# Moving the first key lists into the query projection and changing the pace of gathered rows in a PEER encoder layer

## The chip, the cores and the metric

The kernel runs on one core of a Trainium2 chip, as one launch. The metric is the time of one execution on the device in microseconds (us). A core has a matrix engine (TensorE, in the profile PE, its weight loads PEld), VectorE (DVE), ScalarE (ACT), GpSimd (POOL) and SyncE (SP, used here only to issue transfers), each with an instruction queue of its own that it works off in order, and 16 DMA engines that all transfer queues share.

## What is computed

One layer of an encoder on 512 tokens of width 1024, in float32. Cut to the part that matters here:

```python
h = h + W_out [ DiffAttn(xn) || BiRG-LRU(xn) ]
q = (xn @ wq).reshape(B, S, 8, 2, 64)             # 8 heads, two half keys
s1, s2 = q[..., 0, :] . keys1, q[..., 1, :] . keys2   # 128 scores each
v1, i1 = top_k(s1, 16);  v2, i2 = top_k(s2, 16)
cand = v1[..., :, None] + v2[..., None, :]        # 256 candidates a head
sc, pos = top_k(cand, 16);  g = softmax(sc)
logits = xn . exp_u[idx];  act = gelu(logits) * g # 8 x 16 rows of 16384 experts
h = h + act . exp_v[idx]
h = h + sigmoid(rms(h) W_g) * (p W_p);  out = rms(h)
```

## The kernel before

The 512 tokens are four tiles of 128. A float32 product is made from three matmuls on split operands: `split` (L90 and L92) writes the rounded high part on ACT and the rest on DVE, `mm3` (L97 to L99) issues high x high, high x low, low x high.

The experts are looked up in two ways. Tiles 0 to 2 are **dense**: all 16384 rows of u pass through TensorE in 128 blocks (the first sweep; `u_mm` writes a block's logits `lg`), and then all rows of v in 128 blocks (the second sweep; `v_mm` sums into six PSUM banks `acc`). What makes this right is a weight matrix that is zero but for the chosen experts; it is built from the key lists with one-hot products (`build`, PSUM tile `pg`), written to DRAM as `gd` and read back as `gc` in the second sweep (`weights`, L994: eight parts for a group of eight blocks, 192 KB each). Tile 3 is **gathered**: its 128 rows of u and 128 rows of v for each token are fetched by indirect DMA from POOL (`gather`, L888, 128 rows of 4 KB for one index column), and DVE takes one dot product (L920) or one weighted sum into h (L927) for each. 256 such gathers are spread over both sweeps and the end.

The order is written out by hand. The query projection runs head by head (loop at L864): 24 matmuls a head, the split of the result into `qh`, `ql`, the load and split of the weights two heads ahead. Beside it, two steps of the key lists (`topk`, L687) of tile 3 are issued a head. In `topk`, a head's scores are one PSUM tile `pk`, copied by ACT to `sc`; two steps of five DVE instructions each (L700 to L704) then find the 16 largest of both halves. After the eight heads follow the candidate lists, the softmax (an Exp on ACT, L738), and the arithmetic of the indices. The lists of tiles 0, 1 and 2 follow in the first sweep. There each block calls three generators with a budget in units (`Background.run`): `top` (the lists), `make` (the builds) and `side` (the gathered rows, 1.15 units each):

```python
    for j in range(P):
        advance()                       # row_load up to three blocks ahead
        ...
        u_mm(*ahead.pop(0), lg)
        first = not res[0]              # lists of tile 0 not done yet
        top.run(TOP_FIRST if first else TOP_THEN)
        make.run(MAKE_2 if top.done else MAKE)
        ...
        side.run(SIDE_1 if first else SIDE if not make.done or (vp is not None and parts) else SIDE_2)
```

At block 118 at the latest the build is finished by force, its room is handed on (`settle`), and the first group of `gc` is loaded in four blocks, two parts each. A scheduler then orders the instructions of each engine by their dependencies, so that a line may stand far from its place in the code. At the end `bg.run(1e9)` works off what is left of the gathered rows, before the last part of tile 3 (`finish`).

Of the kernel before, what the change touches and what calls it, by code (L numbers as in the profile page):

```python
# [11 lines left out]
F32 = mybir.dt.float32  # L12
# [4 lines left out]
U32 = mybir.dt.uint32  # L17
# [5 lines left out]
P = 128  # L23
# [3 lines left out]
NT = T // P  # L27
EPS = 1e-6
HEADS = 8
K = 16  # L30
# [9 lines left out]
KEEP = 30  # L40
G_SCALE = 2.0 ** 14
RO_AT = [2, 1, 1, 1, 1, 1, 1, 0, 0, 1, 0, 0, 1, 0, 0, 1, 0, 0, 1, 1, 9]
TOP_FIRST, TOP_THEN, MAKE, SIDE_1, SIDE, BG_V, PREP, SIDE_2 = 1.9, 1.0, 0.57, 0.85, 1.2, 1.2, 60, 2.1
MAKE_2, REST = 0.62, 3
LAST = 3
N_HOT = 13
# [14 lines left out]
def trunk(ctx, tc, x, xT, pT, pos, w_lru, w_qkv, w_out, w_q, keys, wab, w_gate, w_proj,  # L61
          vec, row, ut, u, v, out, dbg=None):
# [26 lines left out]
    def split(src, hi, lo, scale=None):  # L89
        nc.scalar.activation(hi, src, AF.Copy, scale=1.0 if scale is None else scale)  # L90
        if scale is None:
            return nc.vector.tensor_sub(lo, src, hi.bitcast(F32))  # L92
        else:
            return nc.vector.scalar_tensor_tensor(lo, src, scale, hi.bitcast(F32), op0=ALU.mult, op1=ALU.subtract)
# [27 lines left out]
    def wq_load(hd):  # L122
        w = nw.tile([P, DK, P], F32, tag="w", name="w")
        nc.sync.dma_start(w, w_q[hd])
        wh = nw.tile([P, DK, P], R, tag="wh", name="wh")
        wl = nw.tile([P, DK, P], R, tag="wl", name="wl")
        split(w, wh, wl)
        return wh, wl
# [13 lines left out]
    def q_mm(ps, wh, wl, half):  # L142
        ts = slice(0, T) if half is None else slice(half * T // 2, (half + 1) * T // 2)
        for k in range(DK):
            mm3(ps[:, ts], wh[:, k, :], wl[:, k, :], x2h[:, k, ts], x2l[:, k, ts], k == 0, k == DK - 1)

    with ExitStack() as st:
        res = st.enter_context(tc.tile_pool(name="res", bufs=1, reuse_waits="tile"))
# [128 lines left out]
        for ct in range(8):  # L277
# [12 lines left out]
            if ct < 4:  # L290
# [16 lines left out]
                for da in range(4):  # L307
                    i = da * 4 + ct
# [86 lines left out]
        for blk in range(3):  # L395
            accs = []

            for t in range(NT):
                tag = ((), ("ro", "po"), ("tr", None, None, "tr"))[blk][t:t + 1]
# [5 lines left out]
            for k2 in range(4):  # L405
# [5 lines left out]
                for kk in range(2):  # L411
                    k = 2 * k2 + kk
# [235 lines left out]
    def row_load(src):  # L648
        r = up.tile([P, D], F32, tag="r", name="r", bufs=3)
        nc.sync.dma_start(r, src)  # L650
        rh = up.tile([P, D], R, tag="rh", name="rh", bufs=3)
        rl = up.tile([P, D], R, tag="rl", name="rl", bufs=3)
        pace.append(split(r, rh, rl))
        return rh, rl
# [9 lines left out]
    bp = e0.enter_context(tc.tile_pool(name="bp", bufs=1, reuse_waits="tile"))  # L664
# [22 lines left out]
    def topk(t, res):  # L687

        tt = slice(t * P, (t + 1) * P)
        v12 = bp.tile([P, 2, HEADS, K], F32, tag="v12", name="v12", bufs=1)  # L690
        i12 = bp.tile([P, 2, HEADS, K], U32, tag="i12", name="i12", bufs=1)
        for hd in range(HEADS):
            pk = psb.tile([P, 2, P], F32, tag="tr", name="pk", bufs=2)
            mm3(pk, qh[:, hd, tt], ql[:, hd, tt], kh, kl, True, True)
# [161 lines left out]

    res = {t: [] for t in range(NT)}

    def tops():
        for t in list(range(NT - 1, ND_V - 1, -1)) + list(range(ND_V)):  # L860
            yield from topk(t, res[t])

    tg = tops()
    for hd in range(HEADS):  # L864
        if hd + 2 < HEADS:
            wq.append(wq_load(hd + 2))
        if hd < 2:
            ps = pq[hd]
            q_mm(ps, *wq[hd], 1)
        else:  # L870
            ps = psb.tile([P, T], F32, tag=("ro", "po")[hd % 2], name="ps")
            q_mm(ps, *wq[hd], None)
        split(ps, qh[:, hd, :], ql[:, hd, :])
        for _ in range(2 if hd else 0):
            next(tg)
    nx.close()
    bw = e0.enter_context(tc.tile_pool(name="bw", bufs=2, side="right", reuse_waits="tile"))

    pace, after = [], []

    def behind(ins):

# [65 lines left out]
    def builds():  # L948
        for t in range(ND_V):
            while not res[t]:  # L950
                yield None
            yield from build(t, *res[t][0])

    def rest():
        for t in range(ND_V, NT):
            while not res[t]:
                yield None
            yield from rows(uv_items(t))
# [14 lines left out]
                    self.debt -= c  # L973

    top, make, side = Background(tg), Background(builds()), Background(rest())

    JC = 8
    J0 = (P - KEEP) // JC * JC
    order = [(J0 + i) % P for i in range(P)]
    feed = [ut[j].rearrange("p k e -> p (k e)") for j in range(P)] + [v[j * P:(j + 1) * P, :] for j in order]  # L980
    ahead = []
    kept = {}

    def advance():
        while feed and len(ahead) < 3:
            ahead.append(row_load(feed.pop(0)))

    def weights(c, part, vp):

        if part == 0:  # L990
            gcs.append(vp.tile([P, NTB, JC, TB], F32, tag="gc", name="gc"))
        b0, b1 = part * NTB // JC, (part + 1) * NTB // JC
        j = order[c * JC]
        ld_ = nc.sync.dma_start(gcs[-1][:, b0:b1], gd[b0:b1, :, j * TB:(j + JC) * TB].rearrange("b p (j t) -> p b j t", t=TB))  # L994

# [14 lines left out]
    sv = ctx.enter_context(ExitStack())  # L1010
    vp, gcs, built, parts = None, [], None, list(range(JC))
    for j in range(P):
        advance()
        if vp is not None:

# [4 lines left out]
        else:  # L1020
            if j == P - KEEP:
                top.run(1e9)
            i = j - (P - KEEP)
# [154 lines left out]
    bg = Background(side.gen)  # L1178
    prep = Background(prepare())
    advance()  # L1180
    vn = [v_prep(0)]

    for i in range(P - LAST + 1):
        advance()
        if i + 1 < P:
            vn.append(v_prep(i + 1))
        if i == P - JC:
            load_gains()
        if i == P - LAST:
            break  # L1190
        rhl, ahl = ahead.pop(0), vn.pop(0)
        for t in range(ND_V):
            v_mm(i, t, *rhl, *ahl)
        if i >= PREP and not prep.done:
            prep.run(BG_V)
        else:
            bg.run(BG_V)
# [114 lines left out]
```

## Time and profile before

| | |
|---|---|
| median of 3 runs | 1486.02 us (1483.64 to 1488.97) |
| the profiled execution | 1491.43 us, of which the span from first to last instruction 1489.7 |
| PE busy | 1462.2 us, 98% of the span |
| DVE, ACT, POOL busy | 1246.7 us (84%), 737.3 (49%), 375.3 (25%) |
| moved by DMA | 392.64 MB, mean 264 GB/s |
| query projection, first sweep, second sweep | about 250 to 295, 295 to 890, 890 to 1430 us of the span |

Busy time of PE is the union of matmuls that overlap in the pipeline, so short pauses between them don't show in it; they show in the number of matmuls that fall into a stretch, and in what PE waited for. An engine's idle time matters only where PE waits for it.

### The profile page before, as it was taken

What the parts mean: (1) busy time and instruction counts of PE and PEld (TensorE: products, weight loads), DVE (VectorE), ACT (ScalarE), POOL (GpSimd) and SP (SyncE); (2) the same over time, 40 slices, a digit from 0 to 9 for tenths busy, and PEclk for the clock granted to TensorE, in tenths of its full rate; (3) what the DMA queues carried; (4) which work ended last, traced back from release to release, by engine and by line L of the source; (5) the groups of instructions that cost most, each with busy time, mean ns of one, the idle gap of its engine ahead of it and who ended that gap; (6) DMA issues with size and microseconds to landing.
All of it is one profiled execution on the core that took longest, in us unless ns stands there. A gap on an engine that the chain in (4) does not pass through costs nothing.

```text
span 1489.7 us, 22160 instructions
## 1 busy us (share of the span) xinstructions
PE 1462.2 (98%) x7907; PEld 1294.2 (87%) x7907; DVE 1246.7 (84%) x2382; ACT 737.3 (49%) x1059; POOL 375.3 (25%) x320
## 2 busy tenths in 40 slices
PE   9999999999999999999999999999999999999997
PEld 7888678899999999999999997888888888888876
DVE  7686986798999998999888777888887568988896
ACT  7974654253455665556455533333333553333346
POOL 0000000002222263333433352232222004344350
PEclk9999999999999999999999999999999999999999
DMA  7134012158788899888997899899999789999962
GB/s 259 59 97 128 14 62 97 46 166 290 247 289 314 306 338 326 305 320 306 345 360 274 286 364 330 294 332 320 360 359 347 253 267 335 370 375 379 345 205 78
DMA packets 168047, 392.64 MB, mean 264 GB/s; under 512 B 15232, under 2 KB 89728, under 8 KB 164864
## 3 DMA queue, kind: packets, MB, share of 16 engines
q1 hardware_dynamic: 111760, 206.74, 41.0%
q0 software_dynamic: 38464, 140.00, 26.5%
q10 hardware_dynamic: 17712, 44.48, 7.8%
q8 instruction: 62, 1.02, 0.3%
q14 instruction: 49, 0.40, 0.1%
HBM read 344.63 MB, written 46.53 MB: 263 GB/s over the span
## 4 chain that ended last, share of the span: by engine, by line
PE 71%; DVE 14%; issue 5%; DMA 5%; ACT 4%; POOL 1%; SPq 0%; DVEq 0%; POOLq 0%; ACTq 0%
PE acc L99 11%; PE acc L98 11%; PE acc L97 11%; PE psl L97 7%; PE psl L99 7%; PE psl L98 7%; DVE rl L92 3%; PE pg L849 2%; PE ps L97 2%; PE ps L99 2%; PE ps L98 2%; DVE h L927 1%; DMA rr<-in_u_dram,qidx 1%; DMA r<-in_v_dram 1%; DVE rr L920 1%
## 5 line engine op out<-in xcount | busy, mean ns | idle before, releaser
L90 ACT ACTIVATE rh<-r 128x1024 fp32r<-128x1024 f32 x256 | 271.2, 1060 | 460.2 <-PE psl L98 190.2
L92 DVE TENSOR_TENSOR rl<-r,rh 128x1024 fp32r<-128x1024 f32 x256 | 312.4, 1221 | 104.0 <-ACT rh L90 103.3
L97 PE MATMUL psl<-x2h,rh 128*128 128x384 f32 x1024 | 346.8, 339 | 1.1 <-ACT lg L661 0.8
L99 PE MATMUL psl<-x2h,rl 128*128 128x384 f32 x1024 | 343.3, 335 | 2.6 <-DVE rl L92 2.6
L98 PE MATMUL psl<-x2l,rh 128*128 128x384 f32 x1024 | 343.0, 335 | 0.0
L97 PE MATMUL acc<-rh,ah 128*128 128x512 f32 x768 | 299.9, 391 | 2.5 <-ACT ah L90 2.5
L99 PE MATMUL acc<-rh,al 128*128 128x512 f32 x768 | 300.1, 391 | 1.2 <-DVE al L92 1.2
L98 PE MATMUL acc<-rl,ah 128*128 128x512 f32 x768 | 299.6, 390 | 0.0
L888 POOL DMA_INDIRECT rr<-in_u_dram,qidx x84 | 109.0, 1298 | 356.6 <-DVE rl L92 284.9
L99 PEld LDWEIGHTS psl<-x2h,rl 128*128 128x128 f32 x1024 | 192.4, 188 | 3.3 <-DVE rl L92 3.3
L97 PEld LDWEIGHTS psl<-x2h,rh 128*128 128x128 f32 x1024 | 192.2, 188 | 1.6 <-ACT lg L661 1.1
L98 PEld LDWEIGHTS psl<-x2l,rh 128*128 128x128 f32 x1024 | 192.6, 188 | 0.0
L888 POOL DMA_INDIRECT rr<-in_v_dram,qidxv x82 | 123.5, 1507 | 222.6 <-DVE rl L92 185.8
L97 PEld LDWEIGHTS acc<-rh,ah 128*128 128x128 f32 x768 | 144.7, 188 | 33.6 <-ACT ah L90 3.8
L99 PEld LDWEIGHTS acc<-rh,al 128*128 128x128 f32 x768 | 144.5, 188 | 32.7 <-DVE al L92 3.1
L98 PEld LDWEIGHTS acc<-rl,ah 128*128 128x128 f32 x768 | 144.6, 188 | 30.1
L920 DVE CUSTOM_DVE_ANT_0 rr<-rr,xn 128x1024 f32<-128x1024 f32 x84 | 102.0, 1217 | 8.7 <-DMA rr<-in_u_dram,qidx 8.7
L927 DVE SCALAR_TENSOR_TENSOR h<-rr,qg,h 128x1024 f32<-128x1024 f32 x82 | 104.9, 1279 | 0.1
L852 ACT COPY sg<-pg 128x512 f32<-128x512 f32 x96 | 96.0, 1109 | 6.4 <-PE pg L849 5.5
L888 POOL DMA_INDIRECT xn<-in_v_dram,qidxv x46 | 68.6, 1492 | 118.5 <-DVE rl L92 107.9
L90 ACT ACTIVATE ah<-am 128x384 fp32r<-128x384 f32 x128 | 65.6, 513 | 53.9 <-DVE am L1061 27.8
L888 POOL DMA_INDIRECT xn<-in_u_dram,qidx x44 | 62.8, 1427 | 113.0 <-DVE rl L92 82.4
(338 smaller groups left out, 2215.5 us busy)
## 6 DMA issues: line engine op xcount, KB each, us to landing
r<-in_ut_dram SPq DMA_DIRECT2D x128, 512.0 KB, 4.7
r<-in_v_dram SPq DMA_DIRECT2D x128, 512.0 KB, 6.8
gd<-sg ACTq DMA_DIRECT2D x24, 1024.0 KB, 7.8
gc<-gd SPq DMA_DIRECT2D x128, 192.0 KB, 5.0
ld<-lg ACTq DMA_DIRECT2D x98, 192.0 KB, 5.4
lg<-ld SPq DMA_DIRECT2D x98, 192.0 KB, 6.5
w<-in_w_qkv_dram SPq DMA_DIRECT2D x12, 512.0 KB, 3.6
w<-in_w_out_dram SPq DMA_DIRECT2D x8, 512.0 KB, 3.7
```

The source lines that it names most:

```text
L90: nc.scalar.activation(hi, src, AF.Copy, scale=1.0 if scale is None else scale)
L92: return nc.vector.tensor_sub(lo, src, hi.bitcast(F32))
L97: nc.tensor.matmul(ps, lhsT=lh, rhs=rh, start=first, stop=False)
L98: nc.tensor.matmul(ps, lhsT=lh, rhs=rl, start=False, stop=False)
L99: nc.tensor.matmul(ps, lhsT=ll, rhs=rh, start=False, stop=last)
L849: nc.tensor.matmul(pg[:, i - q, :], lhsT=o1[:, i // 2, :, i % 2], rhs=o2[part][:, i // 2, :, i % 2], start=part == 0, stop=part == 1)
L852: nc.scalar.copy(sg[:, :, s0:s0 + 4].rearrange("p j t -> p t j"), pg)
L888: g = nc.gpsimd.indirect_dma_start(out=dst, out_offset=None, in_=table, in_offset=bass.IndirectOffsetOnAxis(ap=idx, axis=0))
L920: behind(nc.vector.tensor_tensor_reduce(rr, rr, xn[:, t, :], 1.0, 0.0, ALU.mult, ALU.add, act[:, k % 16:k % 16 + 1]))
L927: behind(nc.vector.scalar_tensor_tensor(h[:, t, :], rr, qg[:, t, k:k + 1], h[:, t, :], op0=ALU.mult, op1=ALU.add))
```

## The change

The lists of all four tiles get a generator of their own (`tks`). In each of the heads 1 to 7 of the query projection one step of tile 0 is issued behind the two of tile 3; `v12` and `i12` get two buffers so that two tiles can be under way. In the heads 5 to 7 one block of u each is loaded and split (`row_load`), which the first sweep did before. Two budgets change: while tile 0's lists are unfinished a block's share of gathered rows rises from 0.85 to 1.0, and after the builds it falls from 2.1 to 1.6. The work is the same in all.

```diff
-TOP_FIRST, TOP_THEN, MAKE, SIDE_1, SIDE, BG_V, PREP, SIDE_2 = 1.9, 1.0, 0.57, 0.85, 1.2, 1.2, 60, 2.1
+TOP_FIRST, TOP_THEN, MAKE, SIDE_1, SIDE, BG_V, PREP, SIDE_2 = 1.9, 1.0, 0.57, 1.0, 1.2, 1.2, 60, 1.6
@@ topk
-        v12 = bp.tile([P, 2, HEADS, K], F32, tag="v12", name="v12", bufs=1)
-        i12 = bp.tile([P, 2, HEADS, K], U32, tag="i12", name="i12", bufs=1)
+        v12 = bp.tile([P, 2, HEADS, K], F32, tag="v12", name="v12", bufs=2)
+        i12 = bp.tile([P, 2, HEADS, K], U32, tag="i12", name="i12", bufs=2)
@@ before the query projection
+    tks = {t: topk(t, res[t]) for t in range(NT)}
+
     def tops():
         for t in list(range(NT - 1, ND_V - 1, -1)) + list(range(ND_V)):
-            yield from topk(t, res[t])
+            yield from tks[t]
 
     tg = tops()
+    pace, after = [], []
+
+    JC = 8
+    J0 = (P - KEEP) // JC * JC
+    order = [(J0 + i) % P for i in range(P)]
+    feed = [ut[j].rearrange("p k e -> p (k e)") for j in range(P)] + [v[j * P:(j + 1) * P, :] for j in order]
+    ahead = []
+
+    def advance():
+        while feed and len(ahead) < 3:
+            ahead.append(row_load(feed.pop(0)))
+
     for hd in range(HEADS):
...
         for _ in range(2 if hd else 0):
             next(tg)
+        if hd:
+            next(tks[0])
+        if hd >= HEADS - 3:
+            ahead.append(row_load(feed.pop(0)))
```

The moved definitions (`pace`, `JC`, `order`, `feed`, `ahead`, `advance`) are taken out further down. Behind the change the lines of the gathered rows are L937 and L944 (before L920 and L927), that of the `gc` loads L1001 (before L994).

On DVE, in the query projection behind the split of head 1 (`v_2356` holds the lists of tile 3, `v_2374` those of tile 0), the instructions stand so:

```order
 L703 MAX v_2356<-sc 128x8 x2
 L704 MAX_INDEX i_2357<-v_2356,sc 128x8 x2
+L700 MAX v_2374<-sc 128x8 x2
+L701 MAX_INDEX i_2375<-v_2374,sc 128x8 x2
+L702 MATCH_REPLACE sc<-v_2374,sc 128x128 x2
+L703 MAX v_2374<-sc 128x8 x2
+L704 MAX_INDEX i_2375<-v_2374,sc 128x8 x2
 L92 TENSOR_TENSOR wl<-w,wh 128x1024
 L92 TENSOR_TENSOR ql<-ps,qh 128x512
```

A pair of tile 0's steps has come in ahead of the split of the next weights. It comes in at every second head, four times in all. The scheduler makes the seven steps into four full pairs, and they are gone from the first sweep. The three splits of u (`rl`) stand at the same place in both kernels, ahead of the query projection.

On SP's queue, at the end of the first sweep (`r` is a block of u or v, `gc` a part of the weights):

```order
-L650 DMA r<-in_ut_dram 128x1024 x20
-L994 DMA gc<-gd 128x3x128 x6
+L650 DMA r<-in_ut_dram 128x1024 x18
+L1001 DMA gc<-gd 128x3x128 x2
 L650 DMA r<-in_ut_dram 128x1024
-L994 DMA gc<-gd 128x3x128 x2
+L1001 DMA gc<-gd 128x3x128 x2
+L650 DMA r<-in_ut_dram 128x1024
+L1001 DMA gc<-gd 128x3x128 x2
+L650 DMA r<-in_ut_dram 128x1024
+L1001 DMA gc<-gd 128x3x128 x2
 L650 DMA r<-in_ut_dram 128x1024 x3
```

Six parts of `gc` that stood in one piece behind block 123 now stand in pairs, the first behind block 121.

On DVE, around the splits of the blocks 125 to 127 of u (`rl`), before:

```order
L92 TENSOR_TENSOR rl_9135<-r_9132,rh_9134 128x1024
L920 ISA xn_76,act0_69<-xn_76 128x1024
L920 ISA act0_69 128x1
L920 ISA rr_9051,act0_69<-rr_9051,xn_76 128x1024
L920 ISA act0_69 128x1
L92 TENSOR_TENSOR rl_9171<-r_9168,rh_9170 128x1024
L920 ISA rr_9088,act0_69<-rr_9088,xn_76 128x1024
L920 ISA act0_69 128x1
L920 ISA rr_9092,act0_69<-rr_9092,xn_76 128x1024
L920 ISA act0_69 128x1
L92 TENSOR_TENSOR rl_9208<-r_9205,rh_9207 128x1024
```

and behind the change, from the same block on:

```order
L92 TENSOR_TENSOR rl_9144<-r_9141,rh_9143 128x1024
L937 ISA rr_9027,act0_69<-rr_9027,xn_76 128x1024
L937 ISA act0_69 128x1
L92 TENSOR_TENSOR rl_9179<-r_9176,rh_9178 128x1024
L937 ISA xn_76,act0_69<-xn_76 128x1024
L937 ISA act0_69 128x1
L937 ISA xn_76,act0_69<-xn_76 128x1024
L937 ISA act0_69 128x1
L92 TENSOR_TENSOR rl_9217<-r_9214,rh_9216 128x1024
```

Between the splits stand fewer gathered rows. From the split of block 125 of u to that of the fourth block of v there are 12 before and 9 behind the change. In all, 18 rows instead of 19 are left behind the last split of v.

## Rows read from the trace of the kernel before

**Rows 1.** The page: busy time and share of the span.
```profile
PE 1462.2 (98%) x7907; PEld 1294.2 (87%) x7907; DVE 1246.7 (84%) x2382; ACT 737.3 (49%) x1059; POOL 375.3 (25%) x320
```

**Rows 2.** Busy time by stretch: us, PE, PEld, DVE, ACT, POOL (instructions), PEclk, DMA share, GB/s.
```profile
890.00:915.00 25.00, 21.71 (x85) 16.30 (x84) 16.95 (x27) 7.95 (x12) 7.73 (x7) 0.93 0.99 363
915.00:1430.00 515.00, 514.53 (x2272) 425.56 (x2271) 415.54 (x551) 200.01 (x274) 153.68 (x125) 1.00 0.94 328
```

**Rows 3.** What PE waited for, 340 to 860 us (total, times, longest).
```profile
PE psl L99 <- DVE rl L92: 2.6, 2, 1.4
PE pg L849 <- DVE o L834: 1.5, 2, 1.3
PE psl L97 <- ACT lg L661: 0.8, 1, 0.8
```

**Rows 4.** What was waited for around the change of sweeps, 895 to 912 us.
```profile
ACT rh L90 <- DMA r<-in_v_dram: 10.9, 2, 5.5
...
PE acc L97 <- ACT ah L90: 2.1, 2, 1.7
```

**Rows 5.** DVE in order of time, query projection: start, us, instruction [idle before].
```profile
245.99 3.49 DVE L92 TENSOR_TENSOR rl<-r,rh 128x1024 fp32r<-128x1024 f32 x3
...
271.54 1.23 DVE L92 TENSOR_TENSOR wl<-w,wh 128x1024 fp32r<-128x1024 f32 x1 [1.65 <-ACT wh L90]
...
277.36 1.23 DVE L92 TENSOR_TENSOR wl<-w,wh 128x1024 fp32r<-128x1024 f32 x1 [1.65 <-ACT wh L90]
```

**Rows 6.** DVE in order of time, lists of tile 0 in the first sweep.
```profile
344.33 0.48 DVE L700 MAX8 v<-sc 128x8 f32<-128x128 f32 x2
...
346.68 1.20 DVE L920 CUSTOM_DVE_ANT_0 rr<-rr,xn 128x1024 f32<-128x1024 f32 x1
...
347.81 1.22 DVE L92 TENSOR_TENSOR rl<-r,rh 128x1024 fp32r<-128x1024 f32 x1
348.94 0.48 DVE L700 MAX8 v<-sc 128x8 f32<-128x128 f32 x2
```

**Rows 7.** What DVE waited for, 342 to 530 us.
```profile
DVE rr L920 <- DMA rr<-in_u_dram,qidx: 0.8, 1, 0.8
```

**Rows 8.** ACT in order of time, lists of tile 0.
```profile
348.16 1.06 ACT L90 ACTIVATE rh<-r 128x1024 fp32r<-128x1024 f32 x1 [2.85 <-PE psl L98]
...
352.71 1.06 ACT L90 ACTIVATE rh<-r 128x1024 fp32r<-128x1024 f32 x1 [2.85 <-PE psl L98]
...
375.44 1.06 ACT L90 ACTIVATE rh<-r 128x1024 fp32r<-128x1024 f32 x1 [2.85 <-PE psl L98]
...
379.60 1.06 ACT L90 ACTIVATE rh<-r 128x1024 fp32r<-128x1024 f32 x1 [2.72 <-PE psl L98]
...
389.92 0.31 ACT L738 ACTIVATE qg<-qg 128x128 f32<-128x128 f32 x1 [3.05 <-DVE qg L737]
```

**Rows 9.** SP in order of time, end of the first sweep.
```profile
850.41 7.20 SPq L994 DMA_DIRECT2D gc<-gd  x6
857.71 1.94 SPq L650 DMA_DIRECT2D r<-in_ut_dram  x1
```

**Rows 10.** The chain that ended last: start, us, what.
```profile
888.94 15.64 DMA r<-in_v_dram
```

**Rows 11.** The page: DMA issues (KB each, median us to landing).
```profile
r<-in_v_dram SPq DMA_DIRECT2D x128, 512.0 KB, 6.8
```

**Rows 12.** DMA from 885 to 905 us: all, and the gathers' queue.
```profile
DMA packets 3763, 7.68 MB, mean 384 GB/s; under 512 B 296, under 2 KB 2191, under 8 KB 3762
...
q0 software_dynamic: 1306, 4.76, 61.3%
```

**Rows 13.** The end: DVE, ACT in order of time; PE's waits, 1455 to 1490 us.
```profile
1460.17 1.28 DVE L927 SCALAR_TENSOR_TENSOR h<-xn,qg,h 128x1024 f32<-128x1024 f32 x1
...
1461.49 1.06 ACT L1142 ACTIVATE x<-h 128x1024 f32<-128x1024 f32 x1 [0.26 <-DVE h L927]
...
PE gate L97 <- DVE hl L92: 1.4, 1, 1.4
```

More of the change, by code (lines that the diff above doesn't have):

```diff
@@ L875, in trunk @@
             next(tg)
+        if hd:
+            next(tks[0])
+        if hd >= HEADS - 3:
+            ahead.append(row_load(feed.pop(0)))
     nx.close()
     bw = e0.enter_context(tc.tile_pool(name="bw", bufs=2, side="right", reuse_waits="tile"))
-    pace, after = [], []
     def behind(ins):
@@ L975, in trunk @@
     top, make, side = Background(tg), Background(builds()), Background(rest())
[L977 to L981, printed above, removed]
     kept = {}
-    def advance():
-        while feed and len(ahead) < 3:
-            ahead.append(row_load(feed.pop(0)))
     def weights(c, part, vp):
```

## The prediction

> **What bounds the kernel now.** I read the busy times first. PE is busy 98% of the span [rows 1], and the change moves PE's work about without removing any, so it can win only time in which PE issues slower than it could. That is found by counting matmuls in stretches. In the quiet second sweep 2272 instructions fall into 515 us, one in 0.227 us; in the 25 us in which the sweeps change hands only 85, where 110 would fit [rows 2]. The 25 that are missing are worth 25 x 0.227 = 5.7 us, with the clock at 0.93 of full speed among the causes. Before that, from 340 to 860 us, PE waited 4.9 us in all: 2.6 for the low part of a block of u, 1.5 for a one-hot operand, 0.8 for a PSUM bank that ACT had not emptied [rows 3]. So the reader is to see a kernel whose front half is even and which has one hole, at the change of sweeps, plus the end.
>
> The hole is a transfer. PE waits for ACT's rounded weights, and ACT for blocks of v, twice, up to 5.5 us [rows 4]: ACT works in order, and the weights that PE needs stand behind the next block's split. The chain that ended last goes through one block of v that was issued at 888.94 and took 15.64 us to land [rows 10], where the median of such a block is 6.8 [rows 11]. From 885 to 905 us the engines move 384 GB/s, and 4.76 of 7.68 MB belong to the gathers [rows 12]. The blocks of v stand in line with the gathered rows of tile 3.
>
> **The change, part by part.**
>
> The splits of three blocks of u: nothing. They stand at the same place of DVE's order and of SP's before and after, and the trace has them in one piece at 246 us, ahead of the query projection [rows 5]. Their cover is the end of the attention stage, which is not touched.
>
> Four pairs of list steps beside the query projection: nothing there. One pair costs DVE 2.35 us, from 344.33 to 346.68 [rows 6]. A head lasts 5.82 us, of which DVE waits 1.65 for ACT [rows 5], so it works 4.2; with a pair at every second head it works 6.5 and 4.2 in turn, 5.3 on the mean. The split that is delayed by 0.7 us is that of weights for the head after the next, and PE reaches those a whole head later. Queued behind the added pair on DVE are that split and the split of the last head's result; on ACT one more copy a pair. If the cover failed, each pair would cost 0.7 us, 2.8 in all. PE's products for four more heads only move: a block with one lasts 4.55 us, without 4.16 [rows 8], so PE spends 1.6 us there and saves them later.
>
> The front of the first sweep: plus 2.0 us. Here DVE is full: from 342 to 530 us it waited once, 0.8 us [rows 7]. A split and a gathered row take it 1.13 us each [rows 6]. Up to the softmax of tile 0 it now has 4 pairs, 4 splits and 2 gathered rows less, 9.4 + 4.5 + 2.3 = 16.2 us; but PE gets there four blocks sooner, 18.2 us. So DVE comes 2.0 us later as seen from PE. PE's 1.6 us in the projection give about 1.0 of that back, the part that DVE doesn't need for the fourth pair. ACT waits 3.05 us for DVE at this Exp [rows 8], and PE's 0.8 us for the bank [rows 3] hang on it; it should wait about 1 us longer. Then one more gathered row than before falls in front of the first build, 1.1 us more, which is paid at the next tight place, the wait for u in the lists of tile 1. Ends: nothing, if the blocks that are split ahead absorb it, and 3.5, if all of 2.0 + 1.1 arrives and a bit of clock with it. I take 2.0, because DVE has no pause in which to catch up.
>
> The change of sweeps: minus 4.7 us. From the split of block 125 of u to the fourth of v, six blocks or 25 us, DVE consumes 9 gathered rows instead of 12, and a gather is issued when DVE frees its buffer. A gather moves as much as a block, 0.524 MB (the same 128 rows of 4 KB) [rows 11]. Wanted before: 6 blocks and 12 gathers, 9.4 MB in 25 us, 378 GB/s, and some 47 GB/s for a part of weights (192 KB) in each block: 425. Delivered: 384 [rows 12]. Wanted after: 315 + 47 = 362. Besides, the six parts of weights that kept SP busy for 7.2 us, with a block of u behind them for 1.94 more [rows 9], now go in pairs from two blocks earlier, so that the stage is entered without arrears. The block that is late need not be punctual: at 15.64 us it cost 4 us of waiting, so about 11 would do. Ends: 5.7 won, if the hole closes, and nothing. I leave 1.0 in it, because the blocks v1 and v2 keep two gathered rows each.
>
> *The page's limit.* The Trainium skill (DMA: Bandwidth & Descriptors, section Where 436 GB/s comes from) gives about 358 GB/s as what HBM grants one core. This trace does not agree, with 384 over 20 us in that stage [rows 12]. By 358 the 362 wanted would still be too many, the term would shrink to about nothing, and the sum would be plus 0.8.
>
> The end: minus 1.2 us. 18 gathered rows are left instead of 19. The last one, 1.28 us at 1460.17, is what the last part of tile 3 waits for on ACT, and PE waits 1.4 us on that path [rows 13]. Ends: 1.2 and nothing.
>
> What PE waits for at the lists of tile 2 and at the builds (2 us or so of rows 3) stays: from the end of tile 0's lists on, budgets and order are the same, three blocks sooner. The second buffer of v12 costs nothing that PE sees.
>
> Sum: 0 + 0 + 2.0 - 4.7 - 1.2 = -3.9 us, on the profiled execution's 1491.43. That execution is 5.4 us above the median of 1486.02, and in part perhaps by this very hole, since nothing else in it varies so easily; I carry the difference over unchanged: 1486.0 - 3.9 = 1482.1 us. A measurement of this kernel can tell about 0.3%, 4.5 us, from no change, so this lies just inside.
>
> **The rivals.**
>
> *The front costs nothing.* PE's waits in 340 to 860 us stay at 4.9, since blocks are split three ahead: -5.9, 1480.1 us. For it: only 0.8 us of PE's waiting hangs on the Exp although ACT waits 3.05 there. Against it: DVE's fullness.
>
> *The hole stays.* The clump of gathers in v0 to v2 is 5 instead of 6, so a transfer limit just under the 362 wanted, or a stall that comes from the clump alone, leaves all of it: 2.0 - 1.2 = +0.8, 1486.8 us. For it: at 890 to 915 us DMA is busy 0.99 and moves 363 [rows 2], so no slack is proven. Against it: the 384 delivered. (The limit that the page gives would lead here.)
>
> *Slower: the hole grows.* Both loads of logits and two gathers now meet the same block of v, since the first two weight products move ahead of the second block's split. If a block of v lands later than before, PE pays the lateness one to one, and half clock for some us after it, as in this hole (0.93). With the front and the end as above the sum stands at +0.8, so the hole must grow by 4.5 - 0.8 = 3.7 us, from 5.7 to 9.4, before the kernel is slower by 0.3%: about 1491 us. Against it: the bytes are fewer.
>
> *The change doesn't do what it says* is true of the splits of u, and priced so.
>
> **How the numbers follow.** The forecast, hole mostly closed and 2 us paid in front: 0.45, its own range 1479 to 1485 (the ends of the front's term), of which nearly half lies beyond 0.3% faster. Front for nothing: 0.25, nearly all faster. Hole stays: 0.21, all same. Hole grows: 0.09. Faster 0.45 x 0.47 + 0.23 = 0.44; same 0.24 + 0.02 + 0.21 = 0.47; slower 0.09. The range reaches from the closed hole with a free front, and 3 us for the spread of the runs shown, 1477, to the hole that stays, with the same added, 1489.5.
>
> **What would show it.** In the changed trace: 25 us around the change of sweeps with over 100 PE instructions and no clock drop, blocks of v landing in under 11 us there; ACT's wait at tile 0's Exp at about 4 us, some 16 us earlier, and PE's waits for u and for banks 2 us more; DVE's waits for ACT in the query projection gone at every second head and PE at the same 5.8 to 6.2 us a head; one gathered row less behind the last split. The prediction is wrong if the hole keeps its 25 matmuls, or if PE's waits in the first sweep move by more than 3.5 us either way.

## The result, and the profile after

| | before | after |
|---|---|---|
| median | 1486.02 us | 1500.8 us (1499.37 to 1503.63) |
| ratio, 95% interval | | 1.0098 (1.0082 to 1.0114) |
| span of the profiled execution | 1489.7 us | 1499.5 us |

The changed kernel is slower by 1.0%, 14.8 us; 1482.1 us had been forecast. The page's busy times answer to [rows 1] and tell nothing of it: PE is busy for the same time, in a longer span.

```profile
PE 1462.9 (98%) x7907; PEld 1293.8 (86%) x7907; DVE 1246.6 (83%) x2382; ACT 736.5 (49%) x1059; POOL 377.0 (25%) x320
```

The same table by stretches as [rows 2], after the change (us, PE, PEld, DVE, ACT, POOL with their instructions, PEclk, DMA share, GB/s), finds the place:

```profile
890.00:915.00 25.00, 25.00 (x113) 20.79 (x112) 21.86 (x32) 8.92 (x13) 10.46 (x9) 1.00 1.03 373
915.00:1125.00 210.00, 210.00 (x928) 173.91 (x927) 173.59 (x235) 76.85 (x105) 55.04 (x53) 1.00 0.96 335
1125.00:1250.00 125.00, 112.72 (x473) 90.79 (x473) 70.92 (x95) 49.04 (x66) 13.82 (x18) 0.95 0.71 237
1250.00:1430.00 180.00, 180.00 (x796) 149.05 (x795) 155.90 (x202) 66.72 (x92) 76.80 (x47) 1.00 1.00 359
```

The hole at the change of sweeps is gone: 113 PE instructions where 85 stood. But from 1125 to 1250 us, in the middle of the sweep that was quiet, there are 473. The kernel before has 549 in the same stretch:

```profile
1125.00:1250.00 125.00, 124.53 (x549) 102.53 (x548) 88.00 (x121) 57.18 (x78) 20.69 (x22) 1.00 0.86 293
```

76 are missing, and 76 x 0.227 = 17.3 us. What PE waited for there, after the change (total, times, longest):

```profile
PE psp L97 <- ACT wg L90: 8.0, 1, 8.0
PE acc L97 <- ACT rh L90: 1.7, 1, 1.7
PE acc L98 <- DVE rl L92: 1.4, 2, 1.0
PE acc L99 <- DVE al L92: 0.8, 1, 0.8
PE psp L98 <- DVE wg L92: 0.5, 1, 0.5
```

These waits make 12.4 us. The rest of the 17 us is put down to half clock behind them (0.95 over 125 us) and to pauses too short for the view. `psp` is the product p W_p, which has nothing to do with the change. Its weights, and then those of the gate, are loaded from POOL's queue (`w`, L1119, L1122 and L1140; before L1112, L1115 and L1133) from block 60 of the second sweep on (`PREP`). POOL in order of time, kernel before (start, us, instruction, in brackets the idle time before it and what ended it):

```profile
1140.15 1.01 POOL L888 DMA_INDIRECT rr<-in_u_dram,qidx  x1 [3.07 <-DVE rl L92]
1141.17 0.60 POOL L1112 DMA_DIRECT2D w<-in_pT_dram  x1
1141.80 0.55 POOL L1115 DMA_DIRECT2D w<-in_w_proj_dram  x1
1150.70 0.54 POOL L1112 DMA_DIRECT2D w<-in_pT_dram  x1 [8.35 <-DMA w<-in_w_proj_dram]
```

and after:

```profile
1117.91 1.01 POOL L905 DMA_INDIRECT xn<-in_u_dram,qidx  x1 [3.07 <-DVE rl L92]
1121.99 1.01 POOL L905 DMA_INDIRECT xn<-in_u_dram,qidx  x1 [3.07 <-DVE rl L92]
1126.07 1.01 POOL L905 DMA_INDIRECT rr<-in_u_dram,qidx  x1 [3.07 <-DVE rl L92]
1130.15 1.01 POOL L905 DMA_INDIRECT rr<-in_u_dram,qidx  x1 [3.07 <-DVE rl L92]
1134.22 1.01 POOL L905 DMA_INDIRECT rr<-in_v_dram,qidxv  x1 [3.07 <-DVE rl L92]
1135.24 0.60 POOL L1119 DMA_DIRECT2D w<-in_pT_dram  x1
1144.01 0.55 POOL L1122 DMA_DIRECT2D w<-in_w_proj_dram  x1 [8.16 <-DVE wg L92]
1150.46 0.54 POOL L1119 DMA_DIRECT2D w<-in_pT_dram  x1 [5.91 <-DVE wg L92]
1156.22 0.53 POOL L1122 DMA_DIRECT2D w<-in_w_proj_dram  x1 [5.22 <-DVE wg L92]
```

Before, the first two loads go out 0.63 us apart; after, each waits until DVE has split the one before it. The chain that ended last runs for some 50 us through seven such single loads of the gate's weights (start, us, what; its first links):

```profile
1192.69 4.74 DMA w<-in_w_gate_dram
1197.45 1.07 ACT wg L90
1198.54 1.24 DVE wg L92
1199.78 0.28 issue
1200.06 5.10 DMA w<-in_w_gate_dram
```

Why there should be one buffer instead of two is in three places of the code:

```python
            extra = [0, 1, 2] if top.done else [0]                   # rows(): three slices of xn
            while n < len(items) and n < i + GBUFS + len(extra) - 1: # GBUFS = 4 buffers "rr"
...
                        w = gp.tile([P, D], F32, tag="rr", name="w") # prepare()
...
        if i >= PREP and not prep.done:
            prep.run(BG_V)                                           # the rows pause meanwhile
        else:
            bg.run(BG_V)
```

Gathered rows go round a ring of seven buffers, four `rr` and three slices of `xn`, and when they pause, five are held by rows that are fetched and not consumed. The weights take `rr` alone. Before, the last five gathers ahead of the weights are xn xn xn rr rr, so that two `rr` are free. The changed kernel has issued one gather more by block 60 (193 to 192 in POOL's order), the last five are xn xn rr rr rr (above), and free are one `rr` and one `xn`. It is the change as a whole that moves the count, and not the budgets alone: with both old budgets and the moved lists (e11) 192 are already issued at block 58.

The front also moved more than forecast. PE's waits from 340 to 860 us, which answer to [rows 3], and ACT at the Exp of tile 0 [rows 8]:

```profile
PE psl L97 <- ACT lg L661: 4.7, 1, 4.7
PE psl L99 <- DVE rl L92: 1.3, 1, 1.3
```
```profile
375.11 0.31 ACT L738 ACTIVATE qg<-qg 128x128 f32<-128x128 f32 x1 [7.33 <-DVE qg L737]
375.32 1.04 ACT L90 ACTIVATE rh<-r 128x1024 fp32r<-128x1024 f32 x1
376.38 1.28 ACT L661 ACT_TABLE_LOAD   x1
377.68 0.49 ACT L661 ACTIVATE lg<-psl 128x384 f32<-128x384 f32 x1
```

ACT waits 7.33 us for DVE instead of 3.05, and PE 4.7 for the bank that the last of these rows empties.

### The profile page after: what moved, and what is told of

Its sections match the earlier page's. It is cut to its first block, busy times and chain, and to the rows that moved or that the text cites. A ratio compares the mean times of both kernels' runs of the same rounds, so it can differ in the third digit from the quotient of the medians.

```text
span 1499.5 us, 22162 instructions
## 1 busy us (share of the span) xinstructions
PE 1462.9 (98%) x7907; PEld 1293.8 (86%) x7907; DVE 1246.6 (83%) x2382; ACT 736.5 (49%) x1059; POOL 377.0 (25%) x320
## 5 line engine op out<-in xcount | busy, mean ns | idle before, releaser
L905 POOL DMA_INDIRECT rr<-in_v_dram,qidxv x82 | 127.0, 1549 | 199.0 <-DVE rl L92 180.7
L937 DVE CUSTOM_DVE_ANT_0 rr<-rr,xn 128x1024 f32<-128x1024 f32 x84 | 102.1, 1219 | 8.8 <-issue 6.9
L944 DVE SCALAR_TENSOR_TENSOR h<-rr,qg,h 128x1024 f32<-128x1024 f32 x82 | 104.9, 1279 | 0.4 <-DMA rr<-in_v_dram,qidxv 0.4
L92 DVE TENSOR_TENSOR al<-am,ah 128x384 fp32r<-128x384 f32 x128 | 70.7, 552 | 21.3 <-ACT ah L90 21.3
```

The costliest lines, as they stand in the source:

```text
L905: g = nc.gpsimd.indirect_dma_start(out=dst, out_offset=None, in_=table, in_offset=bass.IndirectOffsetOnAxis(ap=idx, axis=0))
L937: behind(nc.vector.tensor_tensor_reduce(rr, rr, xn[:, t, :], 1.0, 0.0, ALU.mult, ALU.add, act[:, k % 16:k % 16 + 1]))
L944: behind(nc.vector.scalar_tensor_tensor(h[:, t, :], rr, qg[:, t, k:k + 1], h[:, t, :], op0=ALU.mult, op1=ALU.add))
```

## The experiments

In the runs below the start of the late weights (`PREP`) is moved by a block or two where needed, so that two `rr` are free (the last five gathers of POOL's order tell it); only e2 and e3 leave one free. Ratios are to the kernel before on the same chip, where its median lay between 1486.07 and 1487.52 us; medians of different runs can differ by that much for the chip alone.

| run | what | median us | ratio, 95% interval |
|---|---|---|---|
| e1 | changed, two buffers free | 1483.55 | 0.9989 (0.9976 to 1.0002) |
| e2 | before, one buffer free | 1501.94 | 1.0103 (1.0080 to 1.0126) |
| e3 | changed, a full turn earlier | 1501.68 | 1.0100 (1.0077 to 1.0124) |
| e9 | changed, fetched one row less ahead | 1515.02 | 1.0200 (1.0184 to 1.0217) |
| e4 | changed, SIDE_1 old | 1484.81 | 0.9987 (0.9974 to 0.9999) |
| e8 | before, SIDE_1 new | 1492.99 | 1.0037 (1.0021 to 1.0053) |
| e7 | changed, first rows later | 1479.12 | 0.9952 (0.9933 to 0.9971) |
| e5 | before, SIDE_2 new | 1487.65 | 1.0003 (0.9992 to 1.0013) |
| e6 | changed, SIDE_2 old | 1483.6 | 0.9976 (0.9965 to 0.9988) |
| e11 | changed, both budgets old | 1483.78 | 0.9982 (0.9972 to 0.9993) |
| e10 | e7 with SIDE_2 old | 1479.8 | 0.9954 (0.9941 to 0.9966) |
| e12 | before, first rows later | 1489.57 | 1.0025 (1.0011 to 1.0040) |

### The late weights: e1, e2, e3, e9

e1, on the changed kernel (of this line only `SIDE_1`, the fourth value, `PREP` and `SIDE_2`, the last two, ever differ):

```diff
-TOP_FIRST, TOP_THEN, MAKE, SIDE_1, SIDE, BG_V, PREP, SIDE_2 = 1.9, 1.0, 0.57, 1.0, 1.2, 1.2, 60, 1.6
+TOP_FIRST, TOP_THEN, MAKE, SIDE_1, SIDE, BG_V, PREP, SIDE_2 = 1.9, 1.0, 0.57, 1.0, 1.2, 1.2, 59, 1.6
```

> The changed kernel with the late weights (the projection p W_p and the gate) begun one block of the second sweep earlier, at block 59 instead of 60; one gathered row less has been issued by then, nothing else differs. Theory (ring of buffers): the changed kernel has issued one gather more than the kernel before when these weights begin, five of seven row buffers are held by gathered rows that pause, and of the two that are left only one is of the kind the weights can use instead of two; so each weight waits for the split of the one before it. With one gather less both are free again: PE's wait of 8.0 us at psp and the 5.7 us lost at 1225 to 1250 us go, the first two weights are issued within 1 us of each other, and the time is 1500.8 - 15 = about 1486 us. Rival (the weights are late because transfers crowd at that place): one block earlier changes nothing, 1500 us.

Measured 1483.55 us. POOL in e1, and the stretch of the hole:

```profile
1129.85 1.01 POOL L905 DMA_INDIRECT rr<-in_u_dram,qidx  x1 [3.07 <-DVE rl L92]
1130.86 0.59 POOL L1119 DMA_DIRECT2D w<-in_pT_dram  x1
1131.49 0.55 POOL L1122 DMA_DIRECT2D w<-in_w_proj_dram  x1
1140.22 0.54 POOL L1119 DMA_DIRECT2D w<-in_pT_dram  x1 [8.18 <-DMA w<-in_w_proj_dram]
```
```profile
1125.00:1250.00 125.00, 124.69 (x549) 102.69 (x548) 88.98 (x118) 56.70 (x78) 23.87 (x23) 1.00 0.87 298
```

549 instructions as before the change, and PE waits 0.3 us in all there. One block of advance, a single gathered row, is worth 17 us.

e2, on the kernel before:

```diff
-TOP_FIRST, TOP_THEN, MAKE, SIDE_1, SIDE, BG_V, PREP, SIDE_2 = 1.9, 1.0, 0.57, 0.85, 1.2, 1.2, 60, 2.1
+TOP_FIRST, TOP_THEN, MAKE, SIDE_1, SIDE, BG_V, PREP, SIDE_2 = 1.9, 1.0, 0.57, 0.85, 1.2, 1.2, 61, 2.1
```

> The kernel before with the late weights begun one block later (61 instead of 60), so that one gathered row more has been issued by then: the count of the changed kernel. Theory (ring of buffers): the wait of the changed kernel appears here too, PE waits some 8 us at psp and loses some 5 us again 70 to 90 us later, and the time rises by about 15 us to 1501 us, although no line of the change is in it. Rival (crowded transfers, or something that the moved lists did): unchanged, 1486 us.

The whole loss appears without a line of the change, 15.9 us on the kernel before. POOL and the stretch in e2:

```profile
1138.56 1.01 POOL L888 DMA_INDIRECT rr<-in_v_dram,qidxv  x1 [3.07 <-DVE rl L92]
1139.57 0.60 POOL L1112 DMA_DIRECT2D w<-in_pT_dram  x1
1148.65 0.55 POOL L1115 DMA_DIRECT2D w<-in_w_proj_dram  x1 [8.47 <-DVE wg L92]
```
```profile
1125.00:1250.00 125.00, 113.66 (x481) 90.98 (x481) 72.14 (x96) 49.91 (x69) 13.19 (x18) 0.96 0.72 242
```

e3, on the changed kernel:

```diff
-TOP_FIRST, TOP_THEN, MAKE, SIDE_1, SIDE, BG_V, PREP, SIDE_2 = 1.9, 1.0, 0.57, 1.0, 1.2, 1.2, 60, 1.6
+TOP_FIRST, TOP_THEN, MAKE, SIDE_1, SIDE, BG_V, PREP, SIDE_2 = 1.9, 1.0, 0.57, 1.0, 1.2, 1.2, 53, 1.6
```

> The changed kernel with the late weights begun seven blocks earlier (53 instead of 60): seven gathers less have been issued, a full turn of the ring of seven buffers, so that again one buffer is free. Theory (ring of buffers): the wait stays, some 29 us earlier in the sweep, and the time is that of the changed kernel, about 1500 us (1496 to 1504). Rival (what matters is how early the weights begin, or what else moves at that moment): as with one block earlier or better, about 1486 us.

1501.68 us, with PE's wait at psp some 27 us earlier:

```profile
PE psp L97 <- ACT wg L90: 6.9, 1, 6.9
```

So it is not how early the weights begin; it is where in the ring of seven they begin. The rival of crowded transfers does not fit e1 and e3 together, nor the traffic: from 1150 to 1175 us the DMA engines are busy 0.60 in the changed kernel, and 0.86 in the kernel before.

e9, on the changed kernel:

```diff
-            while n < len(items) and n < i + GBUFS + len(extra) - 1:
+            while n < len(items) and n < i + GBUFS + len(extra) - 2:
```

> The changed kernel with its gathered rows fetched one row less ahead (- 2 for - 1 in the bound of the loop that issues gathers); the late weights stay at block 60, and the rows that are consumed are the same at every place. Theory (ring of buffers): four of the seven row buffers are held when the late weights begin instead of five, two of those that the weights can use are free, the first two weights are issued within 1 us, PE's wait of 8.0 us at psp and the 5.7 us later in the sweep go, and the time falls from 1500.8 to about 1484 us. Rival (the number of rows consumed by then, or the block at which it begins, sets the cost): unchanged, 1500 us; or a row fetched later lands late and costs DVE waits, 1488 us or more.

The theory was right about the ring and wrong about the time; the second rival, rows that land late, came true. The weights still begin at block 60 and the same rows are consumed, but 192 gathers are issued, the first two weights go out at 1162.11 and 1162.69 us, and PE's wait at psp is gone. The time is lost in the first sweep, where rows fetched one later are late. What DVE waited for in e9 from 340 to 860 us:

```profile
DVE rr L937 <- DMA rr<-in_u_dram,qidx: 22.1, 8, 8.1
...
DVE h L944 <- DMA rr<-in_v_dram,qidxv: 17.4, 10, 3.1
```

That is 39.5 us. In the changed kernel DVE waits 9.3 us for rows in the same stretch (6.9 of it put down to no releaser). This kernel can't spare the last row of fetching ahead.

### The softmax of tile 0: e4, e8, e7

e4, on the changed kernel:

```diff
-TOP_FIRST, TOP_THEN, MAKE, SIDE_1, SIDE, BG_V, PREP, SIDE_2 = 1.9, 1.0, 0.57, 1.0, 1.2, 1.2, 60, 1.6
+TOP_FIRST, TOP_THEN, MAKE, SIDE_1, SIDE, BG_V, PREP, SIDE_2 = 1.9, 1.0, 0.57, 0.85, 1.2, 1.2, 61, 1.6
```

> The changed kernel with the share of gathered rows before tile 0's softmax back at 0.85 instead of 1.0 (6 rows ahead of it on DVE instead of 7), and the late weights begun at block 61, where the count of gathers leaves two buffers free. Theory (DVE is late at the softmax by its own work): a row costs 1.13 us, so ACT's wait at the Exp falls from 7.3 to about 6.2 and PE's wait behind it from 4.7 to about 3.6; with the ring's wait gone too the time is about 1 us below that of the run with block 59, 1485 us. Rival (the wait comes from the late landing of the first gathered rows alone): PE's wait there stays at 4.7 or moves with the landing, no difference to the run with block 59.

ACT's wait is 6.17 us and PE's 3.9, as the theory has it; but the time is not below e1's, since other small waits come at the builds (PE waits there for `pg` 1.6 us).

e8, on the kernel before:

```diff
-TOP_FIRST, TOP_THEN, MAKE, SIDE_1, SIDE, BG_V, PREP, SIDE_2 = 1.9, 1.0, 0.57, 0.85, 1.2, 1.2, 60, 2.1
+TOP_FIRST, TOP_THEN, MAKE, SIDE_1, SIDE, BG_V, PREP, SIDE_2 = 1.9, 1.0, 0.57, 1.0, 1.2, 1.2, 58, 2.1
```

> The kernel before with one budget alone changed, SIDE_1 from 0.85 to 1.0 (11 rows instead of 9 ahead of tile 0's softmax), and the late weights begun at block 58, where the count of gathers leaves two buffers free. Theory (DVE is full there and every row is paid): ACT's wait at the Exp rises by 2 x 1.13 us from 3.05 to about 5.3, PE's wait behind it from 0.8 to about 3, 1486 + 2 = 1488 us. Rival (blocks split ahead cover it): PE's wait stays near 1 us, 1486 us.

ACT's wait is 5.37 us, to 0.1 as expected, and PE's 2.2. The closeness is in part luck: with the old SIDE_1 and the lists in the old place ACT's wait is 3.05 us in the kernel before, but 3.71 in e2 and 4.55 in e5, and PE's 0.8, 1.5 and 2.3. So this one profile doesn't set the two rows apart at the softmax. The time does: 1492.99 us, by the ratio 5.5 above the kernel before and not 2. The rows seem to be paid again at the next places where PE waits for DVE (the wait for `rl` in the first sweep is 4.1 us instead of 2.6).

e7, on the changed kernel: the first row is consumed two rows later. The first four gathers are issued where they were; in the trace the fifth goes out at 344.84 us, where it stood at 338.72.

```diff
+            if i == 0:
+                yield 1.15
+                yield 1.15
             rr = got[i]
             if kind == "u":
...
-TOP_FIRST, TOP_THEN, MAKE, SIDE_1, SIDE, BG_V, PREP, SIDE_2 = 1.9, 1.0, 0.57, 1.0, 1.2, 1.2, 60, 1.6
+TOP_FIRST, TOP_THEN, MAKE, SIDE_1, SIDE, BG_V, PREP, SIDE_2 = 1.9, 1.0, 0.57, 1.0, 1.2, 1.2, 61, 1.6
```

> The changed kernel in which the first gathered row is consumed two rows later in the budget (the gathers are issued where they were), the late weights at block 61, where two buffers are free. 5 rows instead of 7 then stand ahead of tile 0's softmax, and DVE has list steps in hand while the first gathers land. Theory (DVE is late at the softmax by the rows and by its wait of 5.9 us for the first two of them): the lateness falls by 2 x 1.13 us and by most of the 5.9, ACT's wait at the Exp falls from 7.3 to about 1 us or none, PE's wait of 4.7 us there goes, and two more rows are left for the end (about 2.5 us): 1483.6 - 5.5 + 2.5 = about 1481 us. Rival (the list steps alone are too slow for four blocks less): PE still waits 3 us or more there, 1484 to 1486 us.

1479.12 us, 0.48% below the kernel before. ACT at the Exp, and all that PE waits for from 340 to 860 us, in e7:

```profile
369.25 0.31 ACT L738 ACTIVATE qg<-qg 128x128 f32<-128x128 f32 x1 [1.99 <-DVE qg L737]
```
```profile
PE ptt L816 <- DVE e L773: 0.9, 1, 0.9
PE pg L849 <- DVE o L834: 0.7, 2, 0.4
```

DVE has no idle time ahead of the first rows any more, and two rows fewer ahead of the Exp; e7 doesn't part the two. In the changed kernel it stood still for them, in order, with list steps behind them:

```profile
340.22 1.23 DVE L937 CUSTOM_DVE_ANT_0 rr<-rr,xn 128x1024 f32<-128x1024 f32 x1 [3.89 <-issue]
...
343.43 1.23 DVE L937 CUSTOM_DVE_ANT_0 rr<-rr,xn 128x1024 f32<-128x1024 f32 x1 [1.98 <-DMA rr<-in_u_dram,qidx]
```

### The change of sweeps and the end: e5, e6, e11, e10, e12

e5, on the kernel before:

```diff
-TOP_FIRST, TOP_THEN, MAKE, SIDE_1, SIDE, BG_V, PREP, SIDE_2 = 1.9, 1.0, 0.57, 0.85, 1.2, 1.2, 60, 2.1
+TOP_FIRST, TOP_THEN, MAKE, SIDE_1, SIDE, BG_V, PREP, SIDE_2 = 1.9, 1.0, 0.57, 0.85, 1.2, 1.2, 62, 1.6
```

> The kernel before with one budget alone changed, SIDE_2 from 2.1 to 1.6 (9 gathered rows instead of 12 from the split of block 125 of u to that of the fourth of v, the weights still six in one piece), and the late weights begun at block 62, where the count of gathers leaves two buffers free. Theory (the clump of gathers makes the hole at the change of sweeps): the 6.3 us that PE loses from 875 to 925 us fall to 1 or less, the front stays as before, 1486 - 5 = 1481 us. Rival (the six parts of weights in one piece make it): the hole stays, 1486 us.

The hole closes, and the time is the same. The row of the stretch, and PE's waits from 1430 us on, in e5:

```profile
890.00:915.00 25.00, 25.00 (x112) 20.70 (x111) 21.30 (x34) 9.32 (x14) 8.01 (x7) 1.00 1.01 370
```
```profile
PE turn L1150 <- DVE x L1144: 3.9, 1, 3.9
PE gate L97 <- DVE hl L92: 1.7, 1, 1.7
```

22 rows instead of 19 are left behind the last split, and they take back what the hole gave: PE waits 5.6 us at the end where it waited 1.4 [rows 13], 1.4 us a row.

e6, on the changed kernel:

```diff
-TOP_FIRST, TOP_THEN, MAKE, SIDE_1, SIDE, BG_V, PREP, SIDE_2 = 1.9, 1.0, 0.57, 1.0, 1.2, 1.2, 60, 1.6
+TOP_FIRST, TOP_THEN, MAKE, SIDE_1, SIDE, BG_V, PREP, SIDE_2 = 1.9, 1.0, 0.57, 1.0, 1.2, 1.2, 62, 2.1
```

> The changed kernel with SIDE_2 back at 2.1 (11 gathered rows in those six blocks instead of 9, the weights still in pairs from two blocks earlier), and the late weights begun at block 62, where two buffers are free. Theory (the clump of gathers): 3 to 5 us of the hole at the change of sweeps come back, 1487 to 1489 us. Rival (the weights' place): it stays closed, as in the run with block 59, 1483.6 us.

In this run the rival won: 112 instructions in the 25 us, with 11 gathered rows, and 1483.6 us. Two later runs have the same order of rows and weights there as e6, and get less. The stretch in e6, e11 and e10:

```profile
890.00:915.00 25.00, 25.00 (x112) 20.67 (x112) 21.51 (x26) 9.32 (x13) 7.00 (x7) 1.00 1.02 369
890.00:915.00 25.00, 24.08 (x106) 19.28 (x105) 20.01 (x28) 9.22 (x14) 7.60 (x7) 1.00 1.02 370
890.00:915.00 25.00, 23.10 (x99) 18.16 (x98) 18.47 (x25) 8.89 (x13) 6.87 (x6) 1.00 0.99 354
```

With the weights in one piece and the old SIDE_2 the count is 85 (before), 99 (e2), 96 (e8) and 94 (e12); with pairs and the new SIDE_2 it is 110 to 115 (after, e1, e3, e4, e7). So fewer gathers close the hole, as e5's 112 and these show; the pairs alone close it in one profile of three.

e11, on the changed kernel:

```diff
-TOP_FIRST, TOP_THEN, MAKE, SIDE_1, SIDE, BG_V, PREP, SIDE_2 = 1.9, 1.0, 0.57, 1.0, 1.2, 1.2, 60, 1.6
+TOP_FIRST, TOP_THEN, MAKE, SIDE_1, SIDE, BG_V, PREP, SIDE_2 = 1.9, 1.0, 0.57, 0.85, 1.2, 1.2, 58, 2.1
```

> The changed kernel with both budgets back (SIDE_1 0.85, SIDE_2 2.1), so that only the moved lists and splits are left of the change, and the late weights at block 58, where two buffers are free: 6 rows ahead of the softmax, 17 behind the last split. Theory (the moved lists alone bring the weights of the second sweep in pairs and with that the closed change of sweeps, and the wait at the softmax as well): PE's wait there is 3.9 us as in the run with the old SIDE_1, the hole of 5 us stays closed, 1483 us. Rival (the budgets close it): the hole is back, 1487 us.

1483.78 us, the same as e1 within the intervals: with the ring's wait out, the two budgets together are worth nothing that can be told, and the moved lists make what gain there is. PE's wait at the softmax is 3.4 us where 3.9 was expected, and PE has 106 instructions in the 25 us; 11 gathered rows beside weights in pairs do cost a little.

e10, on e7:

```diff
-TOP_FIRST, TOP_THEN, MAKE, SIDE_1, SIDE, BG_V, PREP, SIDE_2 = 1.9, 1.0, 0.57, 1.0, 1.2, 1.2, 61, 1.6
+TOP_FIRST, TOP_THEN, MAKE, SIDE_1, SIDE, BG_V, PREP, SIDE_2 = 1.9, 1.0, 0.57, 1.0, 1.2, 1.2, 58, 2.1
```

> The kernel whose first gathered row waits two rows (1479.1 us), with SIDE_2 back at 2.1 and the late weights at block 58, where two buffers are free: 11 rows instead of 9 in the six blocks around the change of sweeps, 17 rows instead of 20 behind the last split. Theory (with the weights in pairs the clump of gathers costs nothing, and rows left for the end cost up to 1.28 us each): PE's waits behind 1450 us fall from 2.2 to about 0.7, the change of sweeps stays closed, 1477.6 us. Rival (the clump comes back as a hole): 1481 us or more.

The end is shorter, as expected (PE's wait for the gate's operand is gone, one of 0.5 us is left), and a part of the hole is back (99 instructions, not closed as expected); the sum is that of e7, not the 1.5 us less that was expected.

e12, on the kernel before:

```diff
+            if i == 0:
+                yield 1.15
+                yield 1.15
             rr = got[i]
             if kind == "u":
...
-TOP_FIRST, TOP_THEN, MAKE, SIDE_1, SIDE, BG_V, PREP, SIDE_2 = 1.9, 1.0, 0.57, 0.85, 1.2, 1.2, 60, 2.1
+TOP_FIRST, TOP_THEN, MAKE, SIDE_1, SIDE, BG_V, PREP, SIDE_2 = 1.9, 1.0, 0.57, 0.85, 1.2, 1.2, 61, 2.1
```

> The kernel before, its lists where they were, with the first gathered row consumed two rows later as in the fastest of these kernels, and the late weights at block 61, where two buffers are free. It asks whether the moved lists are needed for that kernel's 1479 us. Theory (the moved lists close the change of sweeps, the later rows only take away what the moved lists cost at the softmax): the hole at the change of sweeps stays, PE's 1 us at the softmax goes, and 21 rows instead of 19 are left for the end: 1486 to 1488 us. Rival (the later rows alone do it): 1480 us.

Slower by 0.25%: the hole stays (94 instructions in its 25 us), 21 rows are left for the end, and PE waits 4.8 us there. So the later rows alone do not give e7's time. How much of the difference the moved lists make is not parted here, since e7 leaves 20 rows for the end and waits only 1.6 us there.

## Why the prediction was wrong, point by point

**The step that failed** is one that isn't in the sum. The text says that "from the end of tile 0's lists on, budgets and order are the same, three blocks sooner", and counts the second sweep as quiet up to the end. The order wasn't the same: the rows came to block 60 one gather further on in their ring. That cost 16 to 17 us, as e1, e2 and e3 show from both sides and e9 at the same block, and none of the rivals was of this kind. The two orders on POOL show the one gather, and the profile of before had the warning: it loads these weights through the same buffers as the rows, its third load waits 8.35 us, and PE already waited 0.4 us at that place, for ACT's `ah`. That is a part with no slack that hangs on a count, and the change alters the count. Neither of the two signs of being wrong that the prediction names came up (the hole closed, and PE's waits in the first sweep moved by 1.1 us); neither looks at the middle of the second sweep.

**The splits of u, the query projection:** nothing, as forecast. DVE's wait for ACT in the projection comes at every second head, 1.45 and 1.43 us at the heads without a pair of tile 0, and is gone at those with one.

**The front:** the sum took +2.0 us. DVE's own work up to the softmax shrank by what was reckoned, 16.2 us (46.4 from the split of block 13 to the arithmetic ahead of the Exp, now 30.2). But DVE entered that stretch late: its second gathered row came at 343.43 us instead of 342.04, with PE 0.9 us earlier, so 2.3 us later as seen from PE. So ACT's wait is 7.33 us and not the 4 that was foretold, and PE's 4.7 with some us at half clock behind it. In return the later waits that were to stay went: PE waits 6.0 us from 340 to 860 us where it waited 4.9. Half clock (PEclk 0.93 from 340 to 390 us) cost it about 2 us more: the block of u behind the wait takes 6.18 us, from 378.22 to 384.40, and one without list products 4.16. So the first sweep lost about 3 us. That the 2.0 forecast comes near is in part luck: the wait at the Exp was taken far too short, and waits that were kept in the sum went away. A row ahead of the Exp costs ACT about 1 us of waiting: with one row fewer it is 6.17 us in e4 and 5.62 in e11, against 6.93 to 7.33 in the four profiles with seven rows and the same fetching ahead (after, e1, e3, e6). e7 is the cure.

**The change of sweeps:** -4.7 us forecast, 28 x 0.227 = 6.4 between the two profiled executions, with the clock at 1.00. The text put the gathers first and the weights second, and the runs bear that order out: fewer gathers were enough alone in e5, the weights in pairs in e6 but not in e10. But the term was sized on one execution whose hole was deeper than others: against e2, with the same order there and 99 instructions, the 110 of e1 are worth 2.5 us. That it is the sum of bytes, as the text had it, is not shown: in these 25 us 373 GB/s are moved, no less than the 363 of before [rows 2]. The Trainium skill's 358 GB/s for a core (DMA: Bandwidth & Descriptors, Where 436 GB/s comes from), by which this term was to vanish, does not agree with this trace either: 373 are moved, and the term did not vanish.

**The end:** -1.2 us forecast; the wait for the gate's operand (1.4) is gone, 0.4 is left in another. Rows behind the last split and PE's waits behind 1430 us, across the runs and without one of 1.1 to 1.2 us that all have: 17 rows 0.5 us (e10), 18 rows 0.4 (after), 19 rows 1.4 (before), 20 rows 1.6 (e7), 21 rows 4.8 (e12), 22 rows 5.6 (e5).

**The sum:** without the ring the change is worth -2.5 us by the medians (e1 against the kernel before, 1483.55 to 1486.07) and -1.6 by the ratio, where -3.9 had been forecast. The interval reaches from -3.6 to +0.3, so this can't be told from nothing. The deep hole of the execution that the sum was made on is part of the difference.

## What to carry to other kernels

Where two streams share a ring of buffers, what the second finds free depends on how far round the first has come, and a change of pace far away shifts that by one: compare the orders not only where the change is, but at each place where a stream pauses and another takes its buffers. Fixing the count at which it starts is what e1 did; buffers of its own might do it too, but no run here tried them. A budget that thins work out at one place piles it up at another: 0.5 less between the sweeps closed a hole of 5 us and gave the same back at the end. And an engine that works in order should not be given the first use of a transfer while other work stands behind it: in e7 two rows of delay were worth some 4 us on e1, more than the change itself, though in e12 the rows left for the end took it back.

## What the runs showed of the hardware that was not expected

PE drops to half clock around a wait of 8.0 us (PEclk 0.80 from 1150 to 1175 us) and of 4.7 us (0.93 over 50 us), but not around those of 0.9 to 1.6 us in the first sweep. Between them the same wait goes both ways: at the softmax, from 375 to 400 us, PEclk is 0.93 with a wait of 2.2 us in e8 and 1.00 with one of 2.3 us in e5. The second of the first five gathered rows kept DVE waiting 0.7 to 1.9 us in four profiles of the kernel before's order and 1.5 to 2.9 us in six of the changed order, though five gathers are issued in a row in all of them. In e9, with four in a row, it was 0.7 us in the changed order. Why is not settled.
